# One-layer streaming encoder, one core: the MLP's down projection by seven products over a moving set of seven pairs of features, with the residual added by accumulating transfers

## The chip, the cores and the metric

The kernel runs on one NeuronCore of a Trainium2 chip. The metric is the device time of one execution in microseconds. Each of the times below is of one whole launch: conditioning, both attention groups, output projection, MLP and the last norm.

The engines are named as in the profile: PE (TensorE, matmuls; PEld its weight loads), DVE (VectorE), ACT (ScalarE), POOL (GpSimd) and SP (SyncE, which issues nearly all transfers here). Each engine works its own instructions in the order in which the program lists them, and waits on semaphores where it needs the result of another.

## What is computed

One layer over 512 prompt and 64 decode positions (576 columns in all), model width 2048, MLP width 8192, float32 throughout:

```python
ada = jnp.einsum('bd,de->be', jax.nn.silu(c), w_ada) + b_ada
sh_a, sc_a, g_a, sh_m, sc_m, g_m = [t[:, None, :] for t in jnp.split(ada, 6, axis=-1)]
u = (_norm(x) * (1.0 + sc_a) + sh_a).astype(x.dtype)
mix, states = mixer(*split_proj(u, w_in, b_forget))
x = layer_norm(ALPHA * x + g_a * jnp.einsum('bse,ed->bsd', mix, w_out), ln_mix_g, ln_mix_b)
u = (_norm(x) * (1.0 + sc_m) + sh_m).astype(x.dtype)
h = jnp.square(jax.nn.relu(jnp.einsum('bsd,df->bsf', u, w_up) + b_up))
x = layer_norm(ALPHA * x + g_m * jnp.einsum('bsf,fd->bsd', h, w_down), ln_mlp_g, ln_mlp_b)
```

The change concerns the last two lines: `w_up` has 2048 x 8192 numbers, `w_down` 8192 x 2048. In blocks of 128 that is 16 x 64 and 64 x 16.

## The kernel before

**Layout.** Activations lie transposed, with 128 features on the partitions and the 576 positions as columns: a block of features is one 128x576 slab. `big` holds the residual stream as 16 slabs, already divided by ALPHA, so that a gated product is simply added to it. `modc[:, G_M]` holds the MLP's gate, also divided by ALPHA, one number per feature for prompt and one for decode positions; columns 512 to 575 belong to decode, so an operation with a gate is cut at 512 (`split_ranges`).

**Three terms.** Each float32 operand is split in two parts that PE multiplies in one pass: ACT casts the raw numbers to a high part (`whi`, `ahi`, `shi`), DVE subtracts it from the raw numbers for the low part (`wlo`, `alo`, `slo`). A product is high x high + high x low + low x high, three matmuls, here mostly of 128x128 weights by 288 columns (half a slab).

**Up projection.** The first 16 of 64 blocks of features (`FP`) are computed plainly, by `up_block`. The other 48 go in 24 pairs through Strassen's scheme (in Winograd's form): two blocks of outputs and two halves of the columns make a 2x2 block product, for which `seven` (L1091 to L1102) issues seven products instead of eight. For each of the eight pairs of input slabs, a step, it issues 7 x 3 = 21 matmuls. The sums of the input slabs (`th`, `tl`) are made once, by `input_sums`. The sums of the weights are made anew for each step: class `Sums` loads two steps' blocks in one 512 KB transfer (`load`, L1041, into `sraw`), DVE makes the sums (`add`, L1050 to L1054), then `make` splits them (ACT L1062, DVE L1063). `make` runs three steps ahead of PE; `sraw` has two buffers, `shi` and `slo` four each.

After eight steps `combine` (L1106 to L1110) reads the seven products from PSUM and leaves four quarter slabs in `z`. PE's next pair reuses the banks: the first product of a pair has a bank of its own (`qd`), the others wait until `combine` has read theirs. `hidden` applies bias, ReLU (ACT, L1114) and the square (DVE, L1115 and L1116); `hidden_out` (L1120) stores the two slabs to DRAM as `hd`, by SP.

**Order.** The program is written down in the order of the calls; `em` (class `Emitter`) inserts work between PE's steps. `em.tick()` counts the steps, `em.after(n, fn)` calls `fn` n ticks later, and `em.side` holds generators that advance by one `yield` for each tick. A tick comes after each step of 21 matmuls here.

**Down projection.** It is plain and runs in five chunks of 12 blocks of features (`CHUNK`, `CHUNKS`) and a last part of four (`down_last`). Chunks alternate between two homes, `ahi`/`alo` and `yh`/`yl`: while one is multiplied, `fetch_all` brings the next chunk's slabs from `hd` into the low part (L1124), and `split` makes the two parts in place (ACT L1128, DVE L1129). Weights come through class `Loads` (three buffers `raw` of 512 KB) and class `Pieces` (L151, L152), each piece with eight blocks. For each chunk and each of the 16 output slabs, 12 x 3 x 2 matmuls go to one accumulator `acc` (two buffers of two banks), and `gated` (L1191) adds the gated result to `big` on DVE, three instructions for each slab (288, 224 and 64 columns). The pools of the up projection (`swx`, `srx`, `tpx`) are closed before the down pools are opened, and the first down weights are asked for after that.

**End.** `down_last` goes over the columns in two parts (256 to 575, then 0 to 255), so that the norm of the first part runs beside the second part's matmuls.

## Time and profile before

| what | value |
|---|---|
| time, median of 3 runs | 2686.51 us (2684.56 to 2690.99) |
| the profiled execution's own time | 2685.19 us |
| its span, first to last instruction | 2683.5 us |
| granted TensorE clock, mean | 0.992 |
| instructions in the span | 48337 |
| DMA moved | 421.08 MB, 157 GB/s over the span |
| weight loads of the up pairs (`sraw`) | 96 of 512 KB |
| weight loads of the down projection (`raw` from `wdn`, `wdl`) | 120 + 8 of 512 KB |
| stores of the hidden slabs from pairs (`hd` from `z`) | 48 of 288 KB |
| transfers issued by GpSimd | none |

The busy rows of the profile give each engine's busy time and its share of the span. The stretches give the same between two moments, with the granted clock and the share of time in which the DMA engines were busy. A group of instructions has its line, engine, operation and names, then the count, the busy time, the mean duration of one in ns, and behind the second bar the idle time of the engine just before them and what ended it. In a timeline, a row has start and duration in us; what stands in brackets is the idle time before it and its releaser. By these views the up pairs run from about 1285 to 1822 us, the down projection from 1834 to about 2645, and the last norm fills the rest.

### The profile page before, as it was taken

The page shows a single profiled execution, that of the slowest core. Times are in us where ns is not written, and L with a number is a line of the kernel's source. Part 1 is how long each engine was busy: PE and PEld are TensorE (multiplying, and loading weights), DVE is VectorE, ACT ScalarE, POOL GpSimd, SP SyncE. Part 2 cuts the span into 40 slices and gives each one's busy share as a digit, 9 for nine tenths or more (in the row PEclk, how much of TensorE's full clock was granted, in tenths as well). Part 3 has the DMA queues.
Part 4 walks back from the last instruction along what each step waited for, and adds up shares of the span by engine and source line. Part 5 has one row for each costly group of instructions (what it writes and reads, how often), then busy time and mean ns, then how long its engine had stood idle before and what let it go on. Part 6 is the DMA issues. An engine that isn't in the chain of part 4 may idle for free.

```text
span 2683.5 us, 48337 instructions
## 1 busy us (share of the span) xinstructions
PE 2624.2 (98%) x19955; PEld 2567.7 (96%) x19955; DVE 1776.1 (66%) x3239; ACT 914.4 (34%) x1377; POOL 227.3 (8%) x281
## 2 busy tenths in 40 slices
PE   8999999999999999999999999998999999999996
PEld 5699999999999999999999999998999999999996
DVE  6478989889888578678788888885333342423246
ACT  2143333333335346465344444443112121211122
POOL 0021111323224000000000000000000000000004
PEclk9999999999999999999999999998999999999998
DMA  9845667666676444555333333445233232423222
GB/s 388 281 139 186 229 210 234 209 215 203 203 228 213 148 156 160 164 174 193 110 121 121 121 122 123 123 137 191 87 107 112 86 133 87 132 87 100 84 87 71
DMA packets 151756, 421.08 MB, mean 157 GB/s; under 512 B 15000, under 2 KB 35800, under 8 KB 150512
## 3 DMA queue, kind: packets, MB, share of 16 engines
q1 hardware_dynamic: 151536, 418.00, 47.0%
q8 instruction: 156, 2.56, 0.4%
q14 instruction: 64, 0.52, 0.1%
HBM read 384.84 MB, written 36.24 MB: 157 GB/s over the span
## 4 chain that ended last, share of the span: by engine, by line
PE 82%; DVE 6%; issue 5%; DMA 3%; POOL 2%; ACT 1%; SPq 0%; POOLq 0%; ACTq 0%; DVEq 0%
PE acc L213 37%; PE acc L215 18%; PE q L1101 6%; PE q L1102 6%; PE q L1100 6%; DVE junk L737 2%; DVE wlo L152 1%; DMA brow<-F_d 1%; PE tr L430 1%; PE tr L1102 1%; PE tr L1101 1%; PE tr L1100 1%; PE tr L277 1%; POOL big L1238 1%; POOL fb L598 1%
## 5 line engine op out<-in xcount | busy, mean ns | idle before, releaser
L213 PE MATMUL acc<-ahi,whi 128*128 128x288 f32 (+2 forms) x3696 | 897.4, 301 | 13.3 <-ACT whi L151 12.6
L215 PE MATMUL acc<-ahi,wlo 128*128 128x288 f32 (+2 forms) x3696 | 874.6, 294 | 3.3 <-DVE wlo L152 3.3
L213 PE MATMUL acc<-alo,whi 128*128 128x288 f32 (+2 forms) x3696 | 875.7, 294 | 0.0
L152 DVE TENSOR_TENSOR wlo<-raw,whi 128x1024 fp32r<-128x1024 f32 x346 | 425.1, 1230 | 377.7 <-ACT whi L151 377.3
L213 PEld LDWEIGHTS acc<-ahi,whi 128*128 128x128 f32 x3696 | 619.6, 188 | 35.6 <-issue 16.9
L215 PEld LDWEIGHTS acc<-ahi,wlo 128*128 128x128 f32 x3696 | 622.3, 188 | 5.2 <-DVE wlo L152 5.2
L213 PEld LDWEIGHTS acc<-alo,whi 128*128 128x128 f32 x3696 | 621.1, 188 | 0.3
L151 ACT CAST whi<-raw 128x1024 fp32r<-128x1024 f32 x346 | 361.7, 1048 | 741.9 <-PE acc L213 694.5
L737 DVE CUSTOM_DVE_ANT_0 junk<-ada,cb 128x512 f32<-128x512 f32 x512 | 366.9, 717 | 39.3 <-DMA ada<-in_wad 26.8
L1062 ACT CAST shi<-sraw 128x896 fp32r<-128x896 f32 x192 | 177.9, 941 | 238.2 <-DVE sraw L1054 196.2
L1191 DVE SCALAR_TENSOR_TENSOR big<-acc,modc,big 128x64 f32<-128x64 f32 (+3 forms) x288 | 103.7, 411 | 222.2 <-PE acc L215 222.2
L1063 DVE TENSOR_TENSOR slo<-sraw,shi 128x896 fp32r<-128x896 f32 x192 | 203.6, 1088 | 70.6 <-ACT shi L1062 47.8
L1101 PE MATMUL q<-alo,shi 128*128 128x288 f32 x576 | 170.3, 296 | 0.0
L1101 PE MATMUL q<-tl,shi 128*128 128x288 f32 x576 | 170.0, 295 | 0.0
L1102 PE MATMUL q<-th,slo 128*128 128x288 f32 x576 | 170.0, 295 | 0.0
L1102 PE MATMUL q<-ahi,slo 128*128 128x288 f32 x576 | 169.8, 295 | 0.0
L1100 PE MATMUL q<-ahi,shi 128*128 128x288 f32 x576 | 169.4, 294 | 0.0
L1100 PE MATMUL q<-th,shi 128*128 128x288 f32 x576 | 169.3, 294 | 0.0
L213 PE MATMUL acc<-yl,whi 128*128 128x288 f32 x768 | 164.8, 296 | 0.0
L215 PE MATMUL acc<-yh,wlo 128*128 128x288 f32 x768 | 163.4, 293 | 0.0
L213 PE MATMUL acc<-yh,whi 128*128 128x288 f32 x768 | 162.4, 293 | 0.0
L287 POOL TENSOR_TENSOR rs<-rs,mhalf 128x3 f32<-128x3 f32 (+2 forms) x6 | 5.3, 888 | 1781.7 <-DVE rs L286 1781.7
(244 smaller groups left out, 3609.3 us busy)
## 6 DMA issues: line engine op xcount, KB each, us to landing
ada<-in_wad SPq DMA_DIRECT2D x192, 512.0 KB, 5.8
raw<-in_wdn SPq DMA_DIRECT2D x120, 512.0 KB, 3.5
raw<-in_win SPq DMA_DIRECT2D x96, 512.0 KB, 4.3
sraw<-in_wst SPq DMA_DIRECT2D x96, 512.0 KB, 3.9
raw<-in_wout SPq DMA_DIRECT2D x64, 512.0 KB, 3.6
raw<-in_wup SPq DMA_DIRECT2D x64, 512.0 KB, 3.9
hd<-z SPq DMA_DIRECT2D x48, 288.0 KB, 4.6
alo<-hd SPq DMA_DIRECT2D x40, 288.0 KB, 4.0
```

Of the source, the lines that this page charges most:

```text
L151: nc.scalar.copy(hi, raw)
L152: nc.vector.tensor_tensor(lo, raw, hi.bitcast(F32), ALU.subtract)
L213: T.matmul(o, whi, x[:, kb, a:b], start=start and x is hi, stop=False, **kw)
L215: T.matmul(o, wlo, hi[:, kb, a:b], start=False, stop=stop, **kw)
L277: T.transpose(ps[:, i * P : (i + 1) * P], src[:, 4 * g + i, c0 : c0 + P], ident)
L737: V.tensor_tensor_reduce(junk, raw[:, k], cb[:, v], 1.0, 0.0, ALU.mult, ALU.add, parts[:, 2 * l + k, v, q : q + 1],)
L1062: S.copy(hi, raw[:, q % 2, 1:])
L1063: V.tensor_tensor(lo, raw[:, q % 2, 1:], hi.bitcast(F32), ALU.subtract)
L1100: T.matmul(out, wh, xh, start=start, stop=False)
L1101: T.matmul(out, wh, xl, start=False, stop=False)
L1102: T.matmul(out, wl, xh, start=False, stop=stop)
L1191: V.scalar_tensor_tensor(big[:, m, c0:c1], ps[:, i, c0 - a : c1 - a], mod(G_M, m, wh), big[:, m, c0:c1], ALU.mult, ALU.add,)
```

## The change

The down projection now uses the same seven products as the up projection, for 56 of its 64 blocks.

*Pairs and visits.* `ORDER` lists 28 pairs of blocks of hidden features: pairs 8 and 9, then 4 to 7 (blocks 8 to 15, computed plainly), then 10 to 31. `ahi`, `alo`, `th`, `tl` have eight places, each for one pair in seven forms (four quarters and three sums). A visit (32 of them, `VISITS`) multiplies seven pairs (`W`), a window over the places, into one pair of output slabs: visit t takes outputs `2 * (t % 8)` and the next one, over the pairs `window(t)`. From visit to visit the window moves by one pair, except in every eighth; over 32 visits each output pair meets each of the 28 pairs once. While seven places are in use, the eighth is filled with the pair that enters next: `fetch_pair` brings its seven forms from DRAM one tick after the visit's start, and `split_pair` splits them 9 and 11 ticks after it (1152 and 864 columns).

*Blocks left over.* Blocks 0 to 3 (`FIRST`) are multiplied plainly before the visits, 4 to 7 (`LAST`) plainly after them, in two column parts as before. `four_blocks` does both.

*Forms are stored.* A pair's seven forms go to DRAM as one tile `hp` of 128 x 7 x 288: `hidden_sums` makes the three sums and one changed sign on DVE, two ticks after the pair, and one transfer stores all of `z` (now seven quarters) after four ticks. For pairs 4 to 7 the sums are made at their first use (`split_pair`), beside the first plain blocks.

*One stream of weights.* `wst` holds all weights from the up pairs to the end: up pairs, `FIRST`, visits, `LAST`. The order of a step's blocks within `sraw` changes, a third buffer of `sraw` is added (`sr2`), and `add` now comes after the even step's split instead of the odd one's. `Loads`, `Pieces`, `wdn`, `wdl`, `yh`, `yl` and `fetch_all` no longer occur in the down projection.

*Output of a visit.* `combine` as before, now with seven steps between two of them. Then `gates` multiplies the four quarters by the gate on ACT, six instructions in place (`ngm` is the negative gate, for quarters whose sign is changed), and two ticks after the visit `accumulate` has GpSimd issue two transfers of 288 KB from `z` to `big` that add to what stands there. `gated` on DVE remains for the plain blocks.

The diff's core:

```diff
+FIRST = (0, 1, 2, 3)
+LAST = (4, 5, 6, 7)
+W = 7
+ORDER = (8, 9, 4, 5, 6, 7) + tuple(range(10, 32))
+VISITS = 32
+def window(t):
+
+    return range(W * t // 8, W * t // 8 + W)
...
             def add(self):
                 if self.added < self.n // 2:
                     raw = self.raws[self.added]
...
+                    if not self.plain(2 * self.added):
+                        V.tensor_tensor(
+                            raw[:, :, 0:3:2], raw[:, :, 1:4:2], raw[:, :, 2:3].to_broadcast([P, 2, 2, P]), ALU.add
+                        )
+                        V.tensor_tensor(raw[:, :, 5], raw[:, :, 0], raw[:, :, 3], ALU.add)
+                        V.tensor_tensor(raw[:, :, 6], raw[:, :, 4], raw[:, :, 5], ALU.add)
...
+        def hidden_sums():
+
+            V.tensor_tensor(z[:, 2], z[:, 1], z[:, 4], ALU.subtract)
+            V.tensor_tensor(z[:, 4], z[:, 5], z[:, 4], ALU.subtract)
+            V.scalar_tensor_tensor(z[:, 6], z[:, 2], -1.0, z[:, 5], ALU.mult, ALU.subtract)
+            V.scalar_tensor_tensor(z[:, 0], z[:, 6], -1.0, z[:, 3], ALU.mult, ALU.subtract)
...
+            late.append(lambda f=2 * k: hidden(f))
+            em.after(2, hidden_sums)
+            em.after(4, lambda k=k: nc.sync.dma_start(hp[k], z))
...
+        def next_pair(x):
+            parts = split_pair(x)
+            em.after(1, lambda: fetch_pair(x))
+            for n in (2, 4):
+                em.after(W + n, lambda: next(parts))
...
+        def gates(m):
+            for s_, i, g in ((1, 0, modc[:, G_M]), (4, 0, modc[:, G_M]), (3, 1, ngm), (5, 1, ngm)):
+                for c0, c1, wh in split_ranges(*HALVES[s_ in (4, 5)]):
+                    x = z[:, s_, c0 % HN : c1 - c0 + c0 % HN]
+                    S.mul(x, x, g[:, m + i, wh : wh + 1])
...
+                G.dma_start(big[:, m + i].rearrange("p (a b) -> p a b", a=2), x, accum_op=ALU.add)
...
+        for t in range(VISITS):
...
+            qs, banks = new_banks()
+            for i, x in enumerate(window(t)):
+                ahead(i == W - 1)
+                run_late()
+                seven(x % 8, DOWN, next_w(), banks, i == 0, i == W - 1)
                 em.tick()
...
+            combine(*qs)
+            sums.make(n_q[0] + 3)
+            m = 2 * (t % 8)
+            late.append(lambda m=m: gates(m))
+            em.after(2, lambda m=m: accumulate(m))
```

**Place 1: DVE in an up pair.** The rows from the second low part behind a `combine` on, in DVE's order. Before, L1063 makes a low part, L1115 and L1116 are the squares, L1050 to L1054 the sums of the weights:

```order
L1063 TENSOR_TENSOR slo_17634<-sraw_17518,shi_17633 128x896
L1050 TENSOR_TENSOR sraw_17573<-sraw_17573 128x2x256
L1053 TENSOR_TENSOR sraw_17573<-sraw_17573 128x2x128
L1054 TENSOR_TENSOR sraw_17573<-sraw_17573 128x2x128
L1115 TENSOR_TENSOR z<-z 128x288
L1116 TENSOR_TENSOR z<-z 128x864
L1063 TENSOR_TENSOR slo_17668<-sraw_17573,shi_17667 128x896
L1063 TENSOR_TENSOR slo_17693<-sraw_17573,shi_17692 128x896
L1050 TENSOR_TENSOR sraw_17637<-sraw_17637 128x2x256
L1053 TENSOR_TENSOR sraw_17637<-sraw_17637 128x2x128
L1054 TENSOR_TENSOR sraw_17637<-sraw_17637 128x2x128
L1063 TENSOR_TENSOR slo_17725<-sraw_17637,shi_17724 128x896
```

After, the low parts are L1088, the squares L1157 and L1158, the weight sums L1067 to L1071 and `hidden_sums` L1162 to L1165:

```order
L1088 TENSOR_TENSOR slo_17651<-sraw_17479,shi_17650 128x896
L1157 TENSOR_TENSOR z<-z 128x288
L1158 TENSOR_TENSOR z<-z 128x864
L1088 TENSOR_TENSOR slo_17682<-sraw_17535,shi_17681 128x896
L1067 TENSOR_TENSOR sraw_17590<-sraw_17590 128x2x2x128
L1070 TENSOR_TENSOR sraw_17590<-sraw_17590 128x2x128
L1071 TENSOR_TENSOR sraw_17590<-sraw_17590 128x2x128
L1162 TENSOR_TENSOR z<-z 128x288
L1163 TENSOR_TENSOR z<-z 128x288
L1164 SCALAR_TENSOR_TENSOR z<-z 128x288
L1165 SCALAR_TENSOR_TENSOR z<-z 128x288
L1088 TENSOR_TENSOR slo_17714<-sraw_17535,shi_17713 128x896
```

Four operations of 288 columns have come in behind the second set of weight sums, and one low part now stands between the last set's end and the squares.

**Place 2: SP in an up pair.** L1041 is a load of weights, L1120 a store of a hidden slab:

```order
L1041 DMA sraw_17637<-in_wst 128x2x512
L1041 DMA sraw_17696<-in_wst 128x2x512
L1120 DMA hd_12879<-z 256x1x288
L1120 DMA hd_12880<-z 256x1x288
L1041 DMA sraw_17753<-in_wst 128x2x512
L1041 DMA sraw_17808<-in_wst 128x2x512
L1041 DMA sraw_17872<-in_wst 128x2x512
```

After, L1057 is the load and L1267 the store of a pair's seven forms:

```order
L1057 DMA sraw_17590<-in_wst 128x2x512
L1057 DMA sraw_17654<-in_wst 128x2x512
L1057 DMA sraw_17717<-in_wst 128x2x512
L1267 DMA hp_15266<-z 128x2016
L1057 DMA sraw_17773<-in_wst 128x2x512
L1057 DMA sraw_17828<-in_wst 128x2x512
```

One store of 128x2016 stands where two slabs of 288 KB stood, again between loads of weights.

**Place 3: DVE and ACT in the down projection.** Before, DVE makes a weight's low part (L152), adds the gated result (L1191) and splits a fetched slab (L1129):

```order
L152 TENSOR_TENSOR wlo_23821<-raw_23652,whi_23820 128x1024
L1191 SCALAR_TENSOR_TENSOR big<-acc_23769,modc,big 128x288
L1191 SCALAR_TENSOR_TENSOR big<-acc_23769,modc,big 128x224
L1191 SCALAR_TENSOR_TENSOR big<-acc_23769,modc,big 128x64
L152 TENSOR_TENSOR wlo_23881<-raw_23710,whi_23880 128x1024
L1129 TENSOR_TENSOR yl<-yl,yh 128x576
L1191 SCALAR_TENSOR_TENSOR big<-acc_23854,modc,big 128x288
L1191 SCALAR_TENSOR_TENSOR big<-acc_23854,modc,big 128x224
L1191 SCALAR_TENSOR_TENSOR big<-acc_23854,modc,big 128x64
```

After, a stretch of a visit from the last instruction of `combine` (L1152) on; L1172 is the low part of the entering pair's four quarters:

```order
L1152 TENSOR_TENSOR z<-z,q_25690 128x576
L1088 TENSOR_TENSOR slo_25899<-sraw_25733,shi_25898 128x896
L1067 TENSOR_TENSOR sraw_25792<-sraw_25792 128x2x2x128
L1070 TENSOR_TENSOR sraw_25792<-sraw_25792 128x2x128
L1071 TENSOR_TENSOR sraw_25792<-sraw_25792 128x2x128
L1088 TENSOR_TENSOR slo_25910<-sraw_25733,shi_25909 128x896
L1088 TENSOR_TENSOR slo_25945<-sraw_25792,shi_25944 128x896
L1067 TENSOR_TENSOR sraw_25849<-sraw_25849 128x2x2x128
L1070 TENSOR_TENSOR sraw_25849<-sraw_25849 128x2x128
L1071 TENSOR_TENSOR sraw_25849<-sraw_25849 128x2x128
L1172 TENSOR_TENSOR alo<-alo,ahi 128x1152
L1088 TENSOR_TENSOR slo_25977<-sraw_25792,shi_25976 128x896
```

The additions to `big` have gone from DVE; low parts, weight sums and the entering pair's splits have come.

ACT before, casting weights (L151) and slabs (L1128):

```order
L1128 CAST ahi<-alo 128x576 x2
L151 CAST whi_25646<-raw_25466 128x1024
L1128 CAST ahi<-alo 128x576
L151 CAST whi_25705<-raw_25529 128x1024
L151 CAST whi_25760<-raw_25588 128x1024
L151 CAST whi_25818<-raw_25650 128x1024
```

ACT after, from the combine's copy (L1148) through the six gates (L1327):

```order
L1148 COPY z<-tr_24836 128x288
L1087 CAST shi_25042<-sraw_24877 128x896
L1087 CAST shi_25053<-sraw_24877 128x896
L1327 ACTIVATE z<-z,modc 128x288
L1327 ACTIVATE z<-z,modc 128x224
L1327 ACTIVATE z<-z,modc 128x64
L1327 ACTIVATE z<-z,ngm 128x288
L1327 ACTIVATE z<-z,ngm 128x224
L1327 ACTIVATE z<-z,ngm 128x64
L1087 CAST shi_25088<-sraw_24936 128x896
L1171 CAST ahi<-alo 128x1152
L1087 CAST shi_25120<-sraw_24936 128x896
```

The gates stand behind two casts of weights and ahead of the next; GpSimd's two transfers wait for them.

More of the change, by code (lines that the diff above doesn't have):

```diff
@@ L1156, in program, with split @@
-        for fn in late:
-            fn()
+        def hidden_sums():
[3 more added lines that the diff above has]
+            V.scalar_tensor_tensor(z[:, 0], z[:, 6], -1.0, z[:, 3], ALU.mult, ALU.subtract)
+        hp = {k: dp.tile([P, 7, HN], F32, name=f"hp{k}") for k in ORDER}
+        def split(hi, lo):
+            raw = lo.bitcast(F32)
+            S.copy(hi, raw)
+            V.tensor_tensor(lo, raw, hi.bitcast(F32), ALU.subtract)
@@ new lines, in homes, with fetch_plain, run_late, next_w @@
+        def homes(p):
+            return [
+                [v[:, 2 * p] for v in (ahi, alo)], [v[:, 2 * p + 1] for v in (ahi, alo)],
+                [v[:, p].rearrange("p a b -> p (a b)")[:, :NT] for v in (th, tl)],
+            ]
+        def fetch_plain(hs, fs):
+            for (_, lo), f in zip(hs, fs):
+                nc.sync.dma_start(lo.bitcast(F32), hd[f])
+        late = []
+        def run_late():
+            while late:
+                late.pop(0)()
+        n_q = [0]
+        def next_w():
+            n_q[0] += 1
+            return sums.parts.pop(n_q[0] - 1)
@@ new lines, in ahead @@
+        def ahead(last):
+            if not last:
+                sums.make(n_q[0] + 4)
+        first = homes(7) + homes(6)[:1]
+        for n, k in enumerate(pairs):
+            qs, banks = new_banks()
+            for i in range(8):
+                p = (i + 6) % 8 if k == pairs[-1] else i
+                ahead(i == 7)
+                run_late()
+                seven(p, UP, next_w(), banks, i == 0, i == 7)
+                em.tick()
+                if k == pairs[-1]:
+                    if i == 1:
+                        fetch_plain(first, FIRST)
+                    if i >= 2:
+                        fetch_pair(i - 2)
+                    if 4 <= i < 8:
+                        late.append(lambda x=first[i - 4]: split(*x))
+            combine(*qs)
[3 more added lines that the diff above has]
+            em.after(4, lambda k=k: nc.sync.dma_start(hp[k], z))
@@ new lines, in first_pairs, with last_blocks @@
+        def first_pairs():
+            yield from wait(5)
+            for x in range(W - 1):
+                yield from split_pair(x)
+                yield from wait(7)
+        def next_pair(x):
[3 more added lines that the diff above has]
+                em.after(W + n, lambda: next(parts))
+        ends = [x % 8 for x in window(VISITS - 1)]
+        last = homes((ends[0] - 1) % 8) + homes(ends[0])[:1]
+        def last_blocks():
+            em.after(1, lambda: fetch_plain(last, LAST))
+            for i, x in enumerate(last):
+                em.after(min(4 + i, 6), lambda x=x: split(*x))
@@ L1222, in affine, with down_last @@
+        with tc.tile_pool(name="fl", bufs=1, side="right", reuse_waits="tile") as flp:
+            mp, stf, mur1 = ln_tiles(flp)
+            kept = []
+            def down_last(k, cols):
+                for m in (2 * k, 2 * k + 1):
+                    if len(kept) == m:
+                        sums.make(n_q[0] + 4)
+                        kept.append(next_w())
+                    four_blocks(m, kept[m], last, cols)
             def affine(eng, g, a, b):
```

284 lines of the change are left out of this document (148 added, 136 removed).

## The prediction

> **What bounds the kernel now.** I read the page first (busy shares, slices, chain of waits), then the busy time by stretches, then the timelines of PE, DVE and SyncE where the Strassen up projection runs and where the down projection starts.
>
> ```profile
> PE 2624.2 (98%) x19955; PEld 2567.7 (96%) x19955; DVE 1776.1 (66%) x3239; ACT 914.4 (34%) x1377; POOL 227.3 (8%) x281
> PE acc L213 37%; PE acc L215 18%; PE q L1101 6%; PE q L1102 6%; PE q L1100 6%; DVE junk L737 2%; DVE wlo L152 1%; DMA brow<-F_d 1%; PE tr L430 1%; PE tr L1102 1%; PE tr L1101 1%; PE tr L1100 1%; PE tr L277 1%; POOL big L1238 1%; POOL fb L598 1%
> 1400.00:1800.00 400.00, 400.00 (x3026) 399.88 (x3026) 327.59 (x469) 166.84 (x199) 0.00 (x0) 1.00 0.39 122
> 1840.00:2600.00 760.00, 760.00 (x5748) 760.00 (x5748) 262.00 (x412) 157.62 (x174) 0.00 (x0) 1.00 0.32 104
> ```
>
> PE is busy 98% of the span and heads the chain. The last two rows (stretch, its length, then PE, PEld, DVE, ACT, POOL, granted clock, DMA share, GB/s) are the Strassen up projection and the plain down projection. In both PE never pauses, at full clock, and one 128x288 matmul takes the same: 400.00/3026 = 760.00/5748 = 0.1322 us. So removed matmuls are worth their full price, as long as nothing else becomes late. DVE is the candidate: 327.59/400 = 82% busy in the up stretch, 262.00/760 = 34% in the down stretch.
>
> **The change, part by part.**
>
> *Matmuls.* Before, the down projection runs 64 blocks x 16 outputs x 2 halves x 3 terms = 6144 matmuls (the last four blocks at widths 320 and 256, which is the same columns). After: eight plain blocks make 768, and 32 visits x 7 pairs x 21 = 4704, in all 5472. That is 672 fewer, x 0.1322 = -88.8 us. The visits use the seven products as the up projection does, so I take its rate for them.
>
> *The seam between up and down.*
>
> ```profile
> 1821.90 0.29 PE L1102 MATMUL q<-ahi,slo 128*128 128x288 f32 x1
> 1834.19 0.85 PE L213 MATMUL acc<-ahi,whi 128*128 128x288 f32 x2 [12.00 <-ACT whi L151]
> ...
> 1839.93 0.60 PE L215 MATMUL acc<-ahi,wlo 128*128 128x288 f32 x2
> 1840.37 0.42 PE L213 MATMUL acc<-ahi,whi 128*128 128x288 f32 x2
> 1827.27 1.18 SPq L1120 DMA_DIRECT2D hd<-z  x2
> 1828.51 10.11 SPq L109 DMA_DIRECT2D raw<-in_wdn  x6
> ```
>
> PE idles 12.00 us, because SyncE issues the first down weights only behind the last pair's hidden stores. Then 24 matmuls take 1840.37 - 1834.19 = 6.18 us in place of 3.17: another 3.0, at about twice the interval. The new kernel takes plain weights from the same running `wst` stream, and blocks 0 to 3, stored long before, are fetched during the last up pair. So this goes: -15.0 us. What is late next is DVE, below.
>
> *DVE in an up pair.* One pair before, in order of time (start, duration, engine, line, names):
>
> ```profile
> 1398.50 0.76 DVE L1107 TENSOR_TENSOR z<-q,z 128x576 f32<-128x576 f32 x1 [0.52 <-PE q L1102]
> ...
> 1400.70 0.75 DVE L1110 TENSOR_TENSOR z<-z,q 128x576 f32<-128x576 f32 x1
> 1401.37 2.08 DVE L1063 TENSOR_TENSOR slo<-sraw,shi 128x896 fp32r<-128x896 f32 x2
> 1403.37 0.68 DVE L1050 TENSOR_TENSOR sraw<-sraw 128x512 f32<-128x512 f32 x1
> ...
> 1404.89 0.45 DVE L1115 TENSOR_TENSOR z<-z 128x288 f32<-128x288 f32 x1
> 1405.27 1.05 DVE L1116 TENSOR_TENSOR z<-z 128x864 f32<-128x864 f32 x1
> ...
> 1420.71 0.76 DVE L1107 TENSOR_TENSOR z<-q,z 128x576 f32<-128x576 f32 x1 [0.52 <-PE q L1102]
> 1399.82 0.29 PE L1100 MATMUL tr<-ahi,shi 128*128 128x288 f32 x1
> 1419.85 0.40 ACT L1106 COPY z<-tr 128x288 f32<-128x288 f32 x1 [2.31 <-PE tr L1102]
> 1408.93 1.28 SPq L1120 DMA_DIRECT2D hd<-z  x2
> ```
>
> A pair lasts 1420.71 - 1398.50 = 22.21 us, 8 steps of 21 x 0.1322 = 2.776. Count from the combine's first instruction (0). It ends at 1401.45, so 2.95; the next pair's sixteenth matmul, which overwrites the banks read last, comes at 1399.82 + 15 x 0.1322 = 1401.80. A combine that is over 0.35 us late stops PE.
>
> From 2.95 to 22.21 DVE has 19.26 us. It needs 8 low parts at 1.04 (2.08 for two), 4 sets of weight sums at 1404.89 - 1403.37 = 1.52, squares 1.43, and new: four operations of 288 columns (`hidden_sums`), at 0.45 each plus some gaps 1.9. Sum 8.32 + 6.08 + 1.43 + 1.9 = 17.7: it fits with 1.5 us to spare. Cost of these operations: nothing, hidden beside PE.
>
> *The hidden store.* Two stores of 288 KB become one of 7 x 288 x 4 x 128 bytes = 1008 KB, and it moves. SyncE issues in order, and the weight load ahead of the store waits for a low part that stands behind `hidden_sums`: 2.95 + 3 x 1.04 + 2 x 1.52 + 1.43 + 1.9 + 1.04 = 13.5, plus 0.6 for the load's own issue (1.28 for two): the store goes out at 14.1, not at 1408.93 - 1398.50 = 10.4. Behind it queue the next weight loads; its own reader is the next combine, whose ScalarE copy writes `z` at 1419.85 - 1398.50 = 21.35.
>
> ```profile
> hd<-z SPq DMA_DIRECT2D x48, 288.0 KB, 4.6
> sraw<-in_wst SPq DMA_DIRECT2D x96, 512.0 KB, 3.9
> big<-in_xT SPq DMA_DIRECT2D x8, 1152.0 KB, 6.7
> ```
>
> No row shows a 1008 KB store. The nearest in size is the 1152 KB load, 6.7 us: lands at 20.8, in time by 0.55. The other end is twice a 288 KB store, 9.2: lands at 23.3, 2 us late, x 23 pairs = 45 us. I stand near the first, with some lateness: +5 (0 to 45).
>
> *First plain blocks and the first six pairs.*
>
> ```profile
> L1191 DVE SCALAR_TENSOR_TENSOR big<-acc,modc,big 128x288 f32<-128x288 f32 x80 | 41.4, 518 | 208.1 <-PE acc L215 208.1
> L1191 DVE SCALAR_TENSOR_TENSOR big<-acc,modc,big 128x224 f32<-128x224 f32 x80 | 35.3, 442 | 0.0
> L1191 DVE SCALAR_TENSOR_TENSOR big<-acc,modc,big 128x64 f32<-128x64 f32 x96 | 26.4, 275 | 0.0
> L690 DVE TENSOR_TENSOR ckl<-ckr,ckh 128x512 fp32r<-128x512 f32 x16 | 11.0, 687 | 3.2 <-ACT ckh L689 3.2
> L1007 DVE TENSOR_TENSOR x<-ahi,alo 128x1152 f32<-128x1152 f32 x8 | 10.8, 1351 | 0.0
> L1023 DVE TENSOR_TENSOR tl<-sums,th 128x864 fp32r<-128x864 f32 x8 | 8.4, 1051 | 0.0
> L1063 DVE TENSOR_TENSOR slo<-sraw,shi 128x896 fp32r<-128x896 f32 x192 | 203.6, 1088 | 70.6 <-ACT shi L1062 47.8
> L1062 ACT CAST shi<-sraw 128x896 fp32r<-128x896 f32 x192 | 177.9, 941 | 238.2 <-DVE sraw L1054 196.2
> L1129 DVE TENSOR_TENSOR alo<-alo,ahi 128x576 fp32r<-128x576 f32 x40 | 29.3, 752 | 1.0 <-ACT ahi L1128 1.0
> ```
>
> PE takes 384 x 0.1322 = 50.8 us here. The rows group instructions by line and form: count, then busy us and mean ns of one, then idle time before. DVE: 16 outputs x (518 + 442 + 275 + 687 ns) = 30.8; two pairs from `hp` at 1351 + 1051 = 4.8; four pairs whose sums must be made (four of 288 columns 1.8, splits of 288, 576, 576 and 576 columns 2.7) = 18; around it squares, sums, one split and the first Strassen weights, some 10. About 63 by means; back to back DVE runs some 5% under its means (2.08 for two low parts against 2 x 1.088), so 60. That is 9 over PE's time; up to three steps of weights made ahead hide part: +7 (0 to 12).
>
> *A visit.* It lasts 7 x 2.776 = 19.43. DVE has 16.48 between two combines, and needs 7 low parts 7.3, three or four sets of sums (4.6 or 6.1), and in most visits the splits of one entering pair, 1.35 + 1.05 less 5% = 2.3: 14.2 or 15.7. So 0.8 us is left in every second visit, 2.3 in the others, beside the 0.35. It fits, narrowly. ScalarE needs far less: seven casts at 0.94, two of 2.0 together for the entering pair, and six gates that I put at 1.9 from the 0.40 us of 288 columns. An error of 6% on DVE would cost about 0.3 us x 32: +10 (0 to 32).
>
> The fetches of an entering pair (two transfers on SyncE) are issued eight steps, 22 us, before its split, and 288 KB come back in 4.0 us (the next row): nothing.
>
> ```profile
> alo<-hd SPq DMA_DIRECT2D x40, 288.0 KB, 4.0
> L627 POOL TENSOR_TENSOR sm<-sm,mone 128x1 f32<-128x1 f32 (+1 forms) x80 | 63.9, 799 | 344.2 <-ACT p L624 324.0 <-PE acc L213 9.0 <-PE tr L646 7.0
> ```
>
> The residual addition leaves DVE. ScalarE's gates end at about 2.95 + one 0.94 cast + 1.9 = 5.8; then GpSimd issues two 288 KB accumulating transfers. `z` is rewritten by the next combine at 19.43, so they have 13.6 us. Behind that wait in DVE's queue stand the low parts of the next steps, for which PE waits. The trace has no accumulating and no GpSimd-issued transfer; two plain stores issued together take 4.6. From below, then, 4.6; from above, reading source and destination and writing, thrice, 13.8. Both ends meet the deadline: cost 0, at the upper end just.
>
> The Trainium skill (DMA: Bandwidth & Descriptors, Anatomy of one DMA) fits 2.0 us plus bytes/436e3 for a transfer issued from GpSimd, an estimate of 2.7 us here; by it the sum is unchanged. No run shows it so far.
>
> *Last blocks.* Same matmuls, norm and tail. Low parts are made per output (687 ns) instead of per two (1.2 us): +2 (0 to 5) for DVE.
>
> *Sum.* The profiled execution has span 2683.5 and time 2685.19, so 1.7 around it; the median is 1.3 higher. 2683.5 - 88.8 - 15.0 + 5 + 7 + 10 + 2 = 2603.7, plus 1.7 = 2605 us. Without any stall: 2581. All upper ends together: 94 more than that, 2675.
>
> **Rivals.**
>
> *1. The hidden store, or DVE in the visits, is late every time.* For it: margins of 0.55 and 0.8 us in schedules of 20. Against: DVE shows idle gaps in each pair, and loads are prefetched. Price: the store alone at its upper end turns 5 into 45, so 2645; with half the visits' bound more, 2650.
>
> *2. The accumulating transfers land too late: slower than before.* Each us beyond the 13.6 (and 0.35) stops DVE at the combine, then PE, in 31 visits. It decides from 2.6 us beyond, landing 16.5 us after issue: 31 x 2.6 = 81 takes 2605 to 2686. One mechanism would: if GpSimd could prepare a transfer only while DVE pauses, DVE, busy over 90%, would first pause long enough at the combine that waits for the transfer itself, and 4.6 + 1.3 for two issues would be added: 31 x 5.9 = 183, 2788 us. For it: DVE has never been this full beside GpSimd in the trace. Against: all DVE rows of a visit are two-operand TENSOR_TENSOR, and where GpSimd computes beside DVE (attention) its idle time is 324.0 of 344.2 us a wait for a ScalarE result (the L627 row).
> The Trainium skill (SBUF — State Buffer, Who interferes with whom) has DVE and GpSimd share one port pair as an exclusive lock: two-port modes block GpSimd wholly, and `tensor_tensor`, which has no such mode, contends with GpSimd's reads only. By that rule the transfers' descriptors, which are writes, pass, and the time stays at 2605; no run shows it yet.
>
> *3. The change doesn't save matmul time,* because seven products cost more each. The 0.1322 in both stretches speaks against it; 2690 if it were so, under 2%.
>
> **How the numbers follow.** Forecast (2582 to 2630): 0.66. Rival 1 (2630 to 2670): 0.18. Rivals 2 and 3: 0.13, most of it beyond 2694. Below 2582: 0.03. The range 2582 to 2655 takes in the forecast and most of rival 1, 0.8 in all. Faster by over 0.3% (8 us, about what a measurement of this kernel can tell from no change): 0.66 + 0.18 + 0.03 = 0.87; within: 0.03; slower: 0.10.
>
> **What would show it.** Some 12 us of idle PE gone at the seam; PE without pause at 0.132 per matmul in the visits; a combine's period of 22.2 us in pairs and 19.4 in visits; waits of the combine for the hidden store or for GpSimd's transfers absent or under 1 us; DVE near 90% in both stretches. I am wrong if the visits' period exceeds 20.5 us, or the pairs' 23.5.

## The result, and the profile after

| | us, median (lowest to highest) | ratio to before, 95% interval |
|---|---|---|
| before, beside these runs | 2686.50 (2684.56 to 2690.99, 4 runs) | |
| with the change | 2599.25 (2598.55 to 2601.97, 4 runs) | 0.9675 (0.9658 to 0.9692) |

The prediction was 2605 us in a range of 2582 to 2655. The profiled execution with the change took 2601.97 us, 1.7 of them outside its span of 2600.3; it is the slowest of the four runs.

First the page of the kernel with the change: busy times, and the transfers that are new.

```profile
PE 2542.1 (98%) x19283; PEld 2485.3 (96%) x19283; DVE 2137.8 (82%) x3772; ACT 1118.9 (43%) x1749; POOL 306.7 (12%) x345
hp<-z SPq DMA_DIRECT2D x24, 1008.0 KB, 6.7
big<-z POOLq DMA_DIRECT2D x64, 288.0 KB, 5.5
```

PE runs 672 matmuls fewer and is still 98% busy. DVE went from 66% to 82%. The 1008 KB store lands in 6.7 us, the accumulating transfers in 5.5.

Then the busy time by stretches (stretch, length, PE, PEld, DVE, ACT, POOL, granted clock, DMA share, GB/s): pairs, first plain blocks, start of the visits, visits.

```profile
1300.00:1820.00 520.00, 519.62 (x3930) 519.36 (x3929) 457.47 (x696) 216.25 (x258) 0.00 (x0) 1.00 0.44 141
1831.24:1845.00 13.76, 13.76 (x92) 13.76 (x93) 13.40 (x25) 7.56 (x10) 0.00 (x0) 0.88 0.99 302
1886.00:1900.00 14.00, 9.66 (x51) 9.38 (x52) 9.45 (x18) 2.26 (x3) 0.00 (x0) 0.63 0.77 265
1900.00:2500.00 600.00, 600.00 (x4535) 600.00 (x4534) 523.07 (x716) 328.26 (x487) 73.97 (x61) 1.00 0.63 169
```

In the pairs PE pauses for 0.4 us in all and in the visits not at all, one matmul takes 520/3930 = 600/4535 = 0.132 us, and DVE is 88% and 87% busy beside it. What was lost lies between them, in the stretches with a clock of 0.88 and 0.63. The waits of PE there (what for, us in all, times, longest):

```profile
PE q L1134 <- DVE big L1275: 6.2, 2, 4.1
PE acc L1285 <- DVE z L1151: 3.6, 1, 3.6
```

Three places of the timeline carry the account: the first matmul of the pairs (before: line 1100; with the change: line 1134), the first of the last blocks (lines 213 and 1285), and the visits' start. The rows give count, shortest, median and longest ns, and the first and last start.

```profile
L1100 PE MATMUL tr<-ahi,shi x192: 294/295/408, 1286.3 to 1819.2; 128*128 128x288 f32 x192
L213 PE MATMUL acc<-ahi,yh x96: 281/309/472, 2598.8 to 2652.1; 128*128 128x320 f32 x48, 128*128 128x256 f32 x48
```
```profile
L1134 PE MATMUL tr<-ahi,shi x416: 289/293/607, 1290.8 to 2512.9; 128*128 128x288 f32 x139
L1285 PE MATMUL acc<-ahi x66: 278/309/469, 2515.7 to 2575.9; 128*128 128x320 f32 x33, 128*128 128x256 f32 x33
```

From the first pair to the last blocks it was 2598.8 - 1286.3 = 1312.5 us, and is 2515.7 - 1290.8 = 1224.9: 87.6 less, of the 103.8 that the removed matmuls and the old seam were put at. What follows takes 84.7 and 84.6. What goes before, with its code unchanged, ended 4.5 us later in this execution (1290.8 against 1286.3); in the twelve traces of the experiments the pairs began at 1287.7 to 1293.3, so part of this is scatter, and whether part of it is not stays open, as there is one trace of before.

Where the missing 16.2 us went, in order of time. At the seam, ScalarE's, SyncE's and PE's rows:

```profile
1817.64 0.60 SPq L1184 DMA_DIRECT2D alo<-hp  x1
...
1818.76 0.43 SPq L1267 DMA_DIRECT2D hp<-z  x1
...
1828.55 0.40 ACT L1148 COPY z<-tr 128x288 f32<-128x288 f32 x1 [4.79 <-DMA hp<-z]
...
1831.24 0.37 PE L1285 MATMUL acc<-ahi,shi 128*128 128x288 f32 x1 [3.60 <-DVE z L1151]
```

The last combine's COPY waited 4.79 us for the hidden store of the pair before. That store was issued at 1818.76, behind the fetch of one pair and ahead of another's, and landed after 1828.5 - 1818.8 = 9.7 us instead of 6.7. PE waited 3.60 us for the combine. At the start of the visits, PE's rows:

```profile
1886.27 0.37 PE L1134 MATMUL q<-ahi,shi 128*128 128x288 f32 x1 [2.09 <-DVE big L1275]
...
1891.75 0.58 PE L1134 MATMUL q<-th,shi 128*128 128x288 f32 x1 [4.06 <-DVE big L1275]
1892.12 0.44 PE L1135 MATMUL q<-tl,shi 128*128 128x288 f32 x1
1892.36 0.44 PE L1136 MATMUL q<-th,slo 128*128 128x288 f32 x1
...
1896.92 0.31 PE L1134 MATMUL q<-th,shi 128*128 128x288 f32 x1
1897.08 0.29 PE L1135 MATMUL q<-tl,shi 128*128 128x288 f32 x1
```

Two waits for the plain outputs, 2.09 and 4.06 us, and then 21 matmuls at intervals of 0.24 instead of 0.132 until 1896.92, which loses 2.4 more. A like spell of 14 matmuls follows the wait of 3.60 and loses 1.5. So 3.6 + 1.5 + 2.1 + 4.1 + 2.4 = 13.7 of the 16.2 have a place; the visits after 1900 lose nothing. Some 2 us of this belong to the one execution that was profiled: in the seven experiments below that leave the seam as it is, PE waited 2.8 to 3.1 us there, and in five of them no slow matmuls followed.

### The profile page after: what moved, and what is told of

Its sections match the earlier page's. It is cut to its first block, busy times and chain, and to the rows that moved or that the text cites. A ratio compares the mean times of both kernels' runs of the same rounds, so it can differ in the third digit from the quotient of the medians.

```text
span 2600.3 us, 48481 instructions
## 1 busy us (share of the span) xinstructions
PE 2542.1 (98%) x19283; PEld 2485.3 (96%) x19283; DVE 2137.8 (82%) x3772; ACT 1118.9 (43%) x1749; POOL 306.7 (12%) x345
## 3 DMA queue, kind: packets, MB, share of 16 engines
q1 hardware_dynamic: 165040, 449.55, 53.1%
q0 software_dynamic: 17408, 18.88, 4.7%
## 4 chain that ended last, share of the span: by engine, by line
PE 79%; DVE 8%; issue 5%; DMA 4%; POOL 3%; ACT 1%; SPq 0%; POOLq 0%; ACTq 0%; DVEq 0%
PE acc L222 18%; PE q L1135 12%; PE q L1136 12%; PE q L1134 12%; PE acc L224 9%; PE tr L1136 2%; PE tr L1135 2%; PE tr L1134 2%; DVE junk L747 2%; DVE wlo L161 1%; DMA ada<-in_wad 1%; PE tr L440 1%; DMA brow<-F_d 1%; PE acc L1285 1%; PE acc L1286 1%
## 5 line engine op out<-in xcount | busy, mean ns | idle before, releaser
L222 PE MATMUL acc<-ahi,whi 128*128 128x288 f32 (+2 forms) x2512 | 642.9, 303 | 2.1 <-ACT whi L160 1.4
L224 PE MATMUL acc<-ahi,wlo 128*128 128x288 f32 (+2 forms) x2512 | 618.5, 294 | 2.9 <-DVE wlo L161 2.8
L222 PE MATMUL acc<-alo,whi 128*128 128x288 f32 (+2 forms) x2512 | 617.8, 293 | 0.0
L1087 ACT CAST shi<-sraw 128x896 fp32r<-128x896 f32 (+1 forms) x432 | 401.3, 930 | 470.2 <-PE q L1135 290.3
L1088 DVE TENSOR_TENSOR slo<-sraw,shi 128x896 fp32r<-128x896 f32 (+1 forms) x432 | 458.8, 1072 | 37.5 <-ACT shi L1087 32.0
L1134 PEld LDWEIGHTS q<-th,shi 128*128 128x128 f32 x1248 | 235.5, 189 | 5.0 <-issue 5.0
L1134 PEld LDWEIGHTS q<-ahi,shi 128*128 128x128 f32 x1248 | 235.3, 189 | 2.4 <-issue 2.3
L1135 PEld LDWEIGHTS q<-alo,shi 128*128 128x128 f32 x1248 | 235.5, 189 | 0.0
L1136 PEld LDWEIGHTS q<-th,slo 128*128 128x128 f32 x1248 | 235.4, 189 | 0.0
L1135 PEld LDWEIGHTS q<-tl,shi 128*128 128x128 f32 x1248 | 235.3, 189 | 0.0
```

What stands on the lines that cost most here:

```text
L222: T.matmul(o, whi, x[:, kb, a:b], start=start and x is hi, stop=False, **kw)
L224: T.matmul(o, wlo, hi[:, kb, a:b], start=False, stop=stop, **kw)
L1087: S.copy(hi, raw)
L1088: V.tensor_tensor(lo, raw, hi.bitcast(F32), ALU.subtract)
L1134: T.matmul(out, wh, xh, start=start, stop=False)
L1135: T.matmul(out, wh, xl, start=False, stop=False)
```

## Experiments

Each time stands against the 2599.25 us of the kernel with the change; the kernel before, run beside them, had medians of 2686.7 to 2688.7. "One run" means a single timed execution with its profile. Runs of one kernel lie up to 6.4 us apart (before the change, 2684.56 to 2690.99), so a difference of a few us between medians is weak by itself; where it matters, the lengths of the stages in the traces stand beside it, each from the first matmul of one stage to the first of the next.

**1. What a matmul of the visits is worth.** The first kernel adds as many matmuls as the change had removed, the next two take some away.

```diff
+            if form is DOWN:
+                T.matmul(out, wh, xh, start=False, stop=False)
+                T.matmul(out, wh, xl, start=False, stop=False)
+                T.matmul(out, wl, xh, start=False, stop=stop)
```


> Each step of a visit repeats the three matmuls of its last product, so the visits have eight products' worth of matmuls again (the last product is counted twice in the output): 32 x 7 x 3 = 672 matmuls more than the changed kernel, as many as the kernel before had. Everything else of the change stays. Theory (the time is PE's, each matmul at 0.1322 us): +88.8 us, so 2688, and DVE's busy share in the visits falls to about 76%. Rival (the visits' period is set by DVE, ScalarE or the transfers, and PE follows with slack): the added matmuls fill that slack, less than +60 us.

One run: 2687.35 us, +88.1, with DVE at 383.77 of 500 us, 77%. So the matmuls alone are worth as much as the whole change gained (what the seam gave and what the new stalls took nearly cancel), and nothing in the visits hides them.

```diff
-                T.matmul(out, wh, xl, start=False, stop=False)
+                if form is UP or f != DOWN[0]:
+                    T.matmul(out, wh, xl, start=False, stop=False)
```


> In the visits the high-by-low term of one of the seven products is left out: 32 x 7 = 224 matmuls fewer; its accuracy is lower. Theory (PE sets the visits' period, DVE fits beside it): -224 x 0.1322 = -29.6 us, so 2570; PE's pauses in the visits stay under 0.1 us. Rival (DVE, at 16.9 us of work in a visit, is the bound already): 0 to -10.

One run: 2574.92 us, -24.3. Most of the 29.6, but not all: in the visits PE now waits for combines seven times, up to 0.4 us and 2.4 in all, where the expectation had pauses under 0.1.

```diff
-                T.matmul(out, wh, xl, start=False, stop=False)
+                if form is UP or f not in (1, 3, 6):
+                    T.matmul(out, wh, xl, start=False, stop=False)
```


> In the visits the high-by-low term of three of the seven products is left out: 672 matmuls fewer; accuracy is lower. PE alone would need 18 x 7 x 0.1322 = 16.66 us in a visit, so -88.8 us. DVE has 523.07/600 of 19.43 = 16.94 us of work in a visit. Theory: DVE now becomes the bound, the period stands at 17.0 to 17.7 instead of 16.66, the gain is 55 to 78 us (2521 to 2544), and DVE is above 95% busy. It also shows GpSimd's accumulating transfers beside a full DVE: by the rival that GpSimd can prepare one only while DVE pauses, they would land far later than the 5.5 us median and the gain would shrink below 40 us.

One run: 2553.43 us, -45.8, less than the theory and more than the rival gave. The stretch of the visits, and the waits of PE in it:

```profile
1900.00:2400.00 500.00, 475.66 (x3502) 467.35 (x3501) 466.25 (x645) 294.48 (x438) 66.93 (x55) 0.99 0.68 182
PE q L1134 <- DVE z L1152: 18.2, 24, 2.2
PE q L1134 <- DVE z L1150: 8.6, 14, 0.8
```

PE now waits for combines in most visits. DVE is 466.25/500 = 93% busy, not full: its second operation of the combine waited 7.5 us in all for GpSimd's transfers, and its weight sums 8.6 us for weights. Per visit, the run before took 0.9 us of matmuls away and 0.8 arrived; this one took 2.8 away and 1.4 arrived. So the visits of the changed kernel are bound by PE with some 1 to 1.4 us to spare in 19.43 (an estimate from these two runs), and below that not DVE's work alone but DVE and the transfers in turn decide. Beside this fuller DVE the accumulating transfers landed after 3.9 to 9.5 us, as before: they are not starved by it.

**2. The residual addition back on DVE.** ScalarE's gates and GpSimd's transfers go.

```diff
-                    S.mul(x, x, g[:, m + i, wh : wh + 1])
+                    V.scalar_tensor_tensor(
+                        big[:, m + i, c0:c1], x, g[:, m + i, wh : wh + 1], big[:, m + i, c0:c1], ALU.mult, ALU.add
+                    )
...
-            em.after(2, lambda m=m: accumulate(m))
```


> The residual addition of the visits goes back to DVE: six operations of 288, 224 and 64 columns on the combined outputs take the place of ScalarE's six gates and of GpSimd's two accumulating transfers. DVE's work in a visit rises from 16.94 us by 2 x (0.45 + 0.40 + 0.27) = about 2.2 to 19.2 of 19.43, and in the visits with an entering pair and four sets of sums beyond the period. Theory (DVE is the narrow engine; the transfers are what makes the visits fit): +5 to +50 us, likeliest +20, so about 2620, with DVE at 97% or more and combines that start late. Rival (GpSimd's path costs PE something that the trace does not name): faster by 5 us or more.

One run: 2610.60 us, +11.4, with DVE at 474.18/500 = 95%. Not all of this is the edit's: in the trace the visits, the only stage that it touches, take 638.4 us in place of 632.1; the rest lies ahead of them or in the scatter of the runs. So the transfers are worth some 6 us, the low end of what was expected: at 95% DVE still keeps up in most visits.

**3. Two deadlines, each pushed.** In the pairs the hidden store one step later:

```diff
-            em.after(4, lambda k=k: nc.sync.dma_start(hp[k], z))
+            em.after(5, lambda k=k: nc.sync.dma_start(hp[k], z))
```


> The hidden store of each pair is issued one step later: on SyncE it then stands behind one more weight load, at about 17.2 us after the combine's start instead of 13.7. With 6.3 to 6.7 us to land that is 23.5 to 23.9, against the next combine's ScalarE copy at 21.36: 2.1 to 2.5 late, of which 0.35 cost nothing. Theory (this store's margin is as narrow as the prediction put it): 23 x 2 = +46 us (25 to 65). Rival (the copy does not depend on it, or SyncE issues in time anyway): under +5.

One run: 2659.73 us, +60.5. Two combines in a row on ScalarE:

```profile
1438.30 0.40 ACT L1148 COPY z<-tr 128x288 f32<-128x288 f32 x1 [5.05 <-DMA hp<-z]
1462.86 0.40 ACT L1148 COPY z<-tr 128x288 f32<-128x288 f32 x1 [5.26 <-DMA hp<-z]
```

The period of a pair is 24.56 us instead of 22.21: 2.35 x 24 = 56 of the 60. The whole stage of the pairs takes 596.0 us in place of 540.5. One step in SyncE's order would have cost two thirds of the gain.

In the visits the gates and the accumulating transfers one to two steps later:

```diff
-            late.append(lambda m=m: gates(m))
-            em.after(2, lambda m=m: accumulate(m))
+            em.after(2, lambda m=m: gates(m))
+            em.after(3, lambda m=m: accumulate(m))
```


> ScalarE's gates, and so GpSimd's two accumulating transfers, are placed two steps later in each visit (some 5.5 us). In the changed kernel the first goes out 4.1 us after the combine's start, the second 0.3 us behind the landing of the first, and the second lands 10 to 15.3 us after the first's issue, so at 14 to 19.4 of the 20.3 us at which the next combine overwrites its source. Theory (the two transfers run one behind the other and their end is a deadline of about 1 us of slack in the heavy visits): the light visits end 0 to 1 us late, the heavy ones 3 to 5 us: +30 to +90 us, with waits of the combine's second DVE operation on GpSimd's transfers. Rival (the transfers overlap, or nothing waits for them): under +5.

One run: 2613.20 us, +14.0. DVE's largest wait for a transfer in the visits:

```profile
DVE z L1150 <- DMA big<-z: 18.9, 16, 2.3
```

The deadline is there: the combine's second operation waited for the transfers in 16 visits, and the visits take 646.1 us in place of 632.1. It was overrun by less than expected. The first transfer went out mostly 7.6 to 9.7 us after the combine's start, where the 4.1 and the 5.5 expected would be 9.6, and from its issue to the second's landing it took 10.4 to 14.2 us, in place of 10.0 to 15.3. That the later transfers met fewer of the entering pairs' fetches would explain the second; it was not tested.

**4. The stalls between pairs and visits.** First two edits that gained nothing, and the two together. The plain fetches and the pair fetches were both put behind the hidden store in the last pair:

```diff
-                    if i == 1:
+                    if i == 3:
                         fetch_plain(first, FIRST)
-                    if i >= 2:
-                        fetch_pair(i - 2)
+                    if i >= 4:
+                        fetch_pair(i - 4)
...
+        fetch_pair(4)
+        fetch_pair(5)
         run_late()
```


> In the last pair the fetches of the plain blocks and of the next pairs are issued two steps later on SyncE, so that the hidden store of the pair before goes out ahead of them; two of the six fetches move behind the last combine. Theory (the 3.60 us wait of PE ahead of the first plain block is that store's late landing, which stops the combine's ScalarE copy): the wait falls under 0.5 us, and the whole becomes 3 to 4.5 us faster, 2595. Rival (the wait is DVE's own work in the last pair, or the moved fetches come too late for the first splits): 0 to +5.

Five runs: 2602.11 us (2600.59 to 2605.90), ratio 0.9687 (0.9674 to 0.9701): no gain, and 2.9 us more by the medians. ScalarE's queue in the last pair:

```profile
1826.04 0.68 ACT L1171 CAST ahi<-alo 128x576 fp32r<-128x576 f32 x1 [5.04 <-DMA alo<-hd]
```

The COPY no longer waits for the store, but the cast ahead of it in ScalarE's queue waits 5.04 us for a plain block that is now fetched too late. The wait had changed its name; the rival was right.

The second edit gave the sums of the four pairs of plainly computed blocks to GpSimd (of a pair's seven forms, three are quarters as they stand and four are sums or differences):

```diff
-            V.tensor_tensor(z[:, 2], raw[1], raw[6], ALU.subtract)
...
+            G.tensor_tensor(z[:, 2], raw[1], raw[6], ALU.subtract)
+            G.tensor_tensor(z[:, 4], raw[5], raw[6], ALU.subtract)
+            G.tensor_tensor(z[:, 0], z[:, 2], raw[5], ALU.add)
+            G.tensor_tensor(z[:, 6], raw[6], raw[1], ALU.subtract)
+            G.tensor_tensor(z[:, 6], z[:, 6], raw[5], ALU.subtract)
+            G.tensor_tensor(z[:, 0], z[:, 0], raw[3], ALU.subtract)
```


> The four sums of each of the first four pairs, made while the plain blocks run, are computed by GpSimd (six operations of 288 columns instead of DVE's four). DVE loses 4 x 1.8 = 7.3 us of work in the stretch of 52 us. Theory (DVE bounds that stretch: the waits of 2.1 and 4.1 us of PE ahead of the first visit's products are DVE's): these waits shrink to under 2 us together, and the slow matmuls behind them go: -5 to -9 us, 2590 to 2594. Rival (GpSimd's operations are late, and ScalarE and DVE wait for them, or something else bounds): 0 to +5.

Four runs: 2606.03 us (2603.70 to 2606.31), ratio 0.9696 (0.9683 to 0.9710): 6.8 us slower. DVE's waits from the pairs on:

```profile
DVE alo L1172 <- POOL z L1207: 13.0, 3, 6.7
```

DVE lost 7.3 us of work and won 13.0 us of waiting: the splits that need GpSimd's six sums stand next in DVE's queue, ahead of the plain outputs for which PE waits. The run shows what it costs to give this work to GpSimd, not what it would be worth if it were gone.

Both of these edits in one kernel, and no other:

> Both edits of this call together. Theory (two separate stalls, each with its own cause): the gains add, -8 to -13 us, 2586 to 2591. Rival (the second stall takes over what the first gives): no more than the larger of the two alone.

Four runs: 2607.84 us (2605.81 to 2610.47), ratio 0.9706 (0.9692 to 0.9719). Neither edit removes a stall, and together they do not either.

The traces of these runs led to two edits of order. The first moves the sixth pair's sums and splits behind the last plain block, without taking any work away:

```diff
-            for x in range(W - 1):
+            for x in range(W - 2):
                 yield from split_pair(x)
...
+        sixth = split_pair(W - 2)
+        next(sixth)
...
+                for n in (1, 2, 3):
+                    em.after(n, lambda: next(sixth, None))
```


> The sums and splits of the sixth pair (5 us of DVE work, 4.1 of it ahead of the last plain outputs in DVE's queue) move behind the last plain block, into the first visit, whose sixth step needs them 14 us after its start. No work is taken away. Theory (PE's waits of 2.1 and 4.1 us at the start of the visits are an order of DVE's queue: the last plain outputs, which free PE's banks, stand behind a pair that is not needed yet, while DVE idles 6.4 us later in the first visit): both waits go, with the some 2 us that the slow matmuls behind them cost: -5 to -8 us, 2592 to 2594. Rival (DVE's total work bounds the stretch up to the first visit's combine, so the wait moves there): -2 to +2.

Five runs: 2595.67 us (2593.19 to 2597.68), ratio 0.9650 (0.9636 to 0.9663), 3.6 us less, between the theory and the rival. Of the two waits one is gone, the other is 2.6 instead of 4.06. So more than half of the stall was DVE's order, and part of it, which I had not expected, is DVE's work: the last plain outputs still end later than PE's last plain block, though DVE runs without a pause up to them.

In the other, only the pair fetches of the last up pair move, with the plain fetches where they were:

```diff
-                    if i >= 2:
-                        fetch_pair(i - 2)
+                    if i >= 4:
+                        fetch_pair(i - 4)
...
+        fetch_pair(4)
+        fetch_pair(5)
         run_late()
```


> In the last up pair the plain blocks are fetched where they were, but the fetches of the first six pairs start two steps later, behind the hidden store of the pair before. Theory (that store, issued at 1818.76 and landing 9.7 us later among those fetches, holds the combine's ScalarE copy for 4.8 us and PE for 3.6): it is issued about 1 us earlier and lands in about 6.7, the wait of PE falls under 1 us: -3 to -4.5 us, 2595 to 2596. Rival (the transfers that are moved are only late in another place, as in the run that moved the plain blocks too): within 1.5 us of the changed kernel.

Four runs: 2596.35 us (2594.64 to 2597.72), ratio 0.9655 (0.9642 to 0.9668), 2.9 us less. PE's waits:

```profile
PE q L1134 <- DVE big L1275: 6.3, 2, 4.2
...
PE acc L1285 <- DVE z L1151: 0.8, 1, 0.8
```

The wait of 3.6 is 0.8, and that of the visits is untouched: two separate causes.

The two orders in one kernel:

> The two orders of this call together. Theory (the two stalls are separate): the gains add up, -7 to -12 us, 2587 to 2592, no wait of PE over 1 us between the pairs and the visits. Rival (the earlier start only meets the DVE backlog sooner): no more than the larger of the two alone.

Four runs: 2592.01 us (2591.48 to 2593.17), ratio 0.9640 (0.9627 to 0.9653), 7.2 us less, near the sum 3.6 + 2.9. The slowest of its runs is 5.4 us below the fastest of the kernel with the change, though the kernel before, run beside them, was 2.2 us slower than beside the change (2688.70 against 2686.50). The lengths of the stages in the four traces say it more plainly than the medians:

| kernel | pairs | first plain blocks | visits |
|---|---|---|---|
| with the change | 540.5 | 52.4 | 632.1 |
| the sixth pair later | 540.6 | 53.5 | 627.4 |
| the pair fetches later | 536.5 | 50.9 | 632.3 |
| both orders | 537.0 | 50.9 | 627.1 |

Each edit shortens its own stage and leaves the other's alone, and both together do what each does alone, within half a microsecond. (The plain blocks differ by the slow matmuls behind PE's wait at the seam, 14 of them in the first row and 23 in the second, none in the others.) This version beats the kernel with the change. Its stretch from the first plain blocks to the visits, below that of the changed kernel:

```profile
1825.00:1890.00 65.00, 56.98 (x413) 56.23 (x412) 57.27 (x117) 26.43 (x42) 0.00 (x0) 0.95 0.67 213
1825.00:1890.00 65.00, 61.77 (x454) 61.37 (x453) 62.56 (x127) 27.77 (x43) 0.00 (x0) 0.97 0.72 238
```

Its mean clock is 0.97, not 0.95, and PE idles 3.2 us in it, not 8.0. One wait of 2.5 us is left, so the expectation of none over 1 us did not come true.

## Why the prediction was right, point by point

**Removed matmuls, -88.8.** Right: the one run with 672 more puts them at 88.1.

**Seam, -15.0.** What was to go went, the 12.00 us and the first weights behind the stores. I wrote that DVE would be late next there. It was a transfer: the hidden store of the pair before, 3.6 us of PE and 1.5 of slow matmuls in the profiled execution, 2.8 to 3.1 of PE in the other traces. I had read the store's margin from a middle pair and not asked what else SyncE issues in the last one.

**Hidden store, +5 (0 to 45).** In the middle pairs it is as worked out. One pair of the kernel with the change, on DVE, SyncE and ScalarE:

```profile
1403.39 0.76 DVE L1149 TENSOR_TENSOR z<-q,z 128x576 f32<-128x576 f32 x1 [1.59 <-PE q L1136]
1417.09 0.59 SPq L1267 DMA_DIRECT2D hp<-z  x1
1424.75 0.40 ACT L1148 COPY z<-tr 128x288 f32<-128x288 f32 x1 [2.31 <-PE tr L1136]
```

Issued at 13.70 after the combine's start (I had 14.1), landed in 6.7 (the same), so at 20.4, ahead of the COPY at 21.36. The +5 was right as a size for another place: nothing in 23 pairs, 3.6 once. The first rival's mechanism is real, as the run with the store one step later shows; its margin held.

**First plain blocks, +7 (0 to 12).** 6.2 us of waits and 2.4 of slow matmuls. The size was right, the reason half right. I added up DVE's work and held it against PE's time. Giving part of DVE's work to GpSimd made it worse, and changing DVE's order alone gained 3.6 (4.7 by the visits' stage): what stands ahead of the plain outputs in DVE's queue decides the greater part, and DVE's work the rest.

**Visits, +10 (0 to 32).** Nothing. The slack was put rightly and was enough: in the trace DVE idles 0.8 us in the tight visits, where I had 0.8, and 2.5 in most others, where I had 2.3. The +10 did not follow from its own working: 6% of 15.7 us is 0.9, which is 0.1 over the 0.8, within the 0.35 that cost nothing. That the slack is narrow shows when PE gets faster: of 29.6 us taken away 24.3 arrive, of 88.8 only 45.8.

**Accumulating transfers, 0.** The cost was right, the working was not. I let the two run side by side, 4.6 to 13.8 us, against 13.6. Two visits on GpSimd, and the first of SyncE's two fetches of an entering pair in each:

```profile
2031.98 1.21 POOL L1331 DMA_DIRECT2D big<-z  x1 [13.96 <-DVE slo L1088]
2041.78 1.22 POOL L1331 DMA_DIRECT2D big<-z  x1 [8.59 <-ACT shi L1087]
2051.45 1.21 POOL L1331 DMA_DIRECT2D big<-z  x1 [8.45 <-ACT z L1327]
2055.70 1.22 POOL L1331 DMA_DIRECT2D big<-z  x1 [3.04 <-DVE sraw L1067]
```
```profile
2032.43 0.59 SPq L1184 DMA_DIRECT2D alo<-hp  x1
...
2054.43 0.61 SPq L1184 DMA_DIRECT2D alo<-hp  x1
```

They run one behind the other: the first of these four landed after 9.5 us, at 2041.46, and the second was issued at 2041.78; the third landed after 3.9, and the fourth followed 0.3 later. A pair takes 10.0 to 15.3 us in all, beyond my upper end. It did no harm for two reasons: the first goes out 4.1 us after the combine's start, not 5.8, and the second's source is overwritten only by the next combine's second operation, at 20.3. That leaves 16.2, so 0.9 us in the worst visit. The second rival had the right place and the wrong cause: what stretches a transfer is the 1008 KB that SyncE fetches half a microsecond behind it (9.5 against 3.9 us), not DVE. All nine transfers of the trace that took 9.3 us or more have such a fetch half a microsecond behind them; beside the fuller DVE of the run with 672 matmuls fewer the longest took 9.5.

The Trainium skill (SBUF — State Buffer, Who interferes with whom) let the descriptors pass beside DVE's two-operand operations; the traces agree, with each issue at 1.2 us and landings of 3.9 us and up also where DVE is 93% busy. The Trainium skill's fit for a transfer issued from GpSimd (DMA: Bandwidth & Descriptors, Anatomy of one DMA), an estimate of 2.7 us, was too low for accumulating ones: the fastest took 3.9.

**Last blocks, +2.** Nothing: 84.7 and 84.6 us.

**The sum.** For stalls I had 24 us and the trace has 16.2. The 4.5 us before the pairs, for which I had no term, take back more than half of that difference, which leaves the profiled 2601.97 us 3 under 2605. The median is 6 under it. The mechanism held, PE full at 0.132 us a matmul, but that the total comes so near is in part luck: the 12 us put on the visits and the last blocks did not come, the 5 put on the store in the pairs were paid once, at the seam, and 4.5 came where no term stood.

## What to carry to other kernels

Where PE is full, removed matmuls are worth their full price as long as the engine beside it keeps a little slack per period; so work out that slack, and look for the loss where one stage hands over to the next. There, ask for each in-order queue what stands ahead of the instruction that the bound engine waits for: reordering two queues gained 7.2 us here, while giving 7.3 us of the busiest one's work to GpSimd lost 6.8. A transfer's margin must be read in the pair in which other transfers are issued beside it, not in a quiet one.

## What the hardware showed that I had not expected

**Accumulating transfers go one at a time.** In all 32 visits the second was issued 0.27 to 0.33 us behind the landing of the first, though its operands were ready up to 9.9 us earlier. Whether the hardware or a semaphore of the program orders them so stays open. They are also dear in DMA time. The page's queues (packets, MB, share of 16 engines):

```profile
q1 hardware_dynamic: 165040, 449.55, 53.1%
q0 software_dynamic: 17408, 18.88, 4.7%
```

The plain queue moved 449.55 MB in 53.1% of the span, 8.5 MB for each per cent; the accumulating one 18.88 in 4.7%, 4.0 MB.

**A pause of PE can cost more than its length.** After the wait of 3.60 us PE soon worked at half its rate for 3.4 us, which cost 1.5 more. At the start of the visits three of the six matmuls behind the wait of 2.09 us were already at 0.24 us, and behind that of 4.06 the rate stayed so for 5.2 us, which cost 2.4 more. The length of the pause does not tell by itself. At the seam nine traces of the experiments have a pause of 2.8 to 3.1 us: no slow spell followed in six (up to 3.07 us), and one of 22 or 23 matmuls in three (3.11 to 3.14). In the version with both orders a pause of 2.46 us at the visits' start had 14 slow matmuls behind it. The Trainium skill (TensorE: Matmul & The Clock Gate, Part 1: The HAM clock gate) says that the clock halves after an idle window of some 3.4 us and comes back after a busy one. The spell of 3.4 us agrees; the slow matmuls behind pauses shorter than 3.4 us do not fit a window that has to be wholly idle, and there the traces decide.

**GpSimd's additions and DVE's slow each other.** In the run with sums on GpSimd one operation of 288 columns took 0.8 us where it had the time for itself, against DVE's 0.45. Where both worked, on GpSimd and on DVE:

```profile
1882.92 0.82 POOL L1205 TENSOR_TENSOR z<-tl,alo 128x288 f32<-128x288 f32 x1
1883.82 1.53 POOL L1206 TENSOR_TENSOR z<-z,tl 128x288 f32<-128x288 f32 x1
1885.31 1.26 POOL L1207 TENSOR_TENSOR z<-z,alo 128x288 f32<-128x288 f32 x1
...
1883.20 1.49 DVE L1088 TENSOR_TENSOR slo<-sraw,shi 128x896 fp32r<-128x896 f32 x1
1884.61 1.28 DVE L1067 TENSOR_TENSOR sraw<-sraw 128x512 f32<-128x512 f32 x1
1885.93 0.92 DVE L1070 TENSOR_TENSOR sraw<-sraw 128x256 f32<-128x256 f32 x1
1886.89 0.42 DVE L1071 TENSOR_TENSOR sraw<-sraw 128x256 f32<-128x256 f32 x1
```

DVE's 1.08, 0.69 and 0.42 us became 1.49, 1.28 and 0.92, and GpSimd's 0.8 became 1.53 and 1.26. The Trainium skill (SBUF — State Buffer, Who interferes with whom) has a DVE instruction with two operands in SBUF contend with a GpSimd instruction that reads SBUF, and these rows agree.
